# One layer of a hybrid decoder trunk: the eight turns of the last residual block ahead of their reading, sums of quarters moved in six blocks, a read of the residual asked for one group later

## The chip, the cores and the metric

The kernel runs on one core of one Trainium2 chip. A core has five engines with queues of their own: TensorE (PE; PEld is its weight load), VectorE (DVE), ScalarE (ACT), GpSimd (POOL) and SyncE (SP), which here issues most DMAs. The metric is the device time of the core in microseconds, the median of several runs.

## The reference, cut to what matters

One layer with 256 positions and 2048 channels, all in float32. The change lies at the end of the first half (output projection and residual) and in the second half (the gated MLP):

```python
def rmsnorm(x, w):
    xf = x.astype(jnp.float32)
    y = xf * lax.rsqrt(jnp.mean(xf * xf, axis=-1, keepdims=True) + EPS)
    return (y * w.astype(jnp.float32)).astype(x.dtype)
...
        mixed = jax.nn.sigmoid(g_a) * y_a + jax.nn.sigmoid(g_b) * y_b
        x = x + jnp.einsum('bsd,de->bse', mixed, w_out[l])

        h = rmsnorm(x, norm_ffn_w[l])
        gate, up = jnp.split(jnp.einsum('bsd,df->bsf', h, w_up[l]), 2, axis=-1)
        gate = causal_dwconv(gate, conv_ffn_w[l]) + conv_ffn_b[l]
        x = x + jnp.einsum('bsf,fd->bsd', jax.nn.gelu(gate, approximate=False) * up, w_down[l])
    return rmsnorm(x, norm_final_w)
```

`w_up` is 2048 x 11264 (5632 columns of gate, 5632 of up), `w_down` 5632 x 2048.

## The kernel before

**Slabs and products.** All weights stream once from memory in slabs of 256 rows by 512 columns (tile 128x2x512, 512 KB). A slab is split for TensorE: ScalarE casts it to a high half (`whi`, L285), VectorE subtracts that from the slab and keeps the rest as low half (`wlo`, L293). A product of a slab is then three kinds of matmuls into a PSUM bank: high weights by high and by low features, then low weights by high features. `weights()` hands out the next slab and first has two more slabs split (`AHEAD = 2`). There are three buffers each of `whi` and `wlo` and four of the raw slab, so a cast waits until the product three slabs back has left its buffer, and a load until the slab four loads back has been split.

**The order.** The list `srcs` fixes the order of slabs for the whole kernel. In the up projection TensorE's order is the one written (`manual_schedule`); ScalarE, VectorE, GpSimd and SyncE are put in order by a scheduler, with hints that one instruction is to come after another (`issue_after`). Each engine then executes its queue in that order. The framework keeps track of dependences by tile: a write into one half of a tile waits for earlier reads of the other half.

**The last residual block.** For each of four column groups `c` the output projection is added to the residual (L1233), and `turned_rows` turns the result: eight 128x128 transposes on TensorE against the identity (L1249), read from PSUM by ScalarE (L1254, high half of the features `fhl`) and VectorE (L1255, low half). For `c == 3` this is done inside the up projection, behind its second product, with one PSUM tile `shared` for all eight turns; there it turns four blocks, reads them in two pairs, turns the other four, reads them. The features so made (k 12 to 15, one tile) are read first by the product of the seventh slab, the fifth product after the turns.

**Blocks of the up projection.** There are eleven column groups `c`, 512 columns of gate and 512 of up. In the groups of `TWO` (1 to 7 and 9) two 1024-row chunks of the gate weights, `ch` 1 and then 0, are multiplied as two by two quarters in seven products instead of eight. The four quarters are loaded into buffers of their own (`quad_load`, L219): b11, b12, b21, b22. Sums of them are made in place by VectorE (L226): T1 = b12 - b11 into b12, T2 = b22 - T1 into b12, T3 = T2 - b11 into b11, T4 = b21 - T2 into b12. The products of a block are called by their operand and their chunk, so 21(0) is the quarter b21 of chunk 0. Around the end of one group they stand in this order, with plain products of the group before between the first ones: T1(1), 11(1), T1(0), 11(0), T2(1), T2(0), 21(1), 21(0), the eight turns of the gate (L1429), T3(1), T3(0), 22(1), 22(0), the eight turns of up, T4(1), T4(0). Two additions by VectorE bring partial results from one PSUM bank into another: L1389 (before 22 begins) and L1403 (before T4 begins). L1324 is the convolution of the gate, ScalarE's L1420 copies finished columns out of PSUM.

**When a sum is made.** `sums_behind` says behind which slab's split a sum is asked for. In the groups of `TWO`, T1(0) and T2(1) are asked for behind 11(1) and the slab after it, T2(0) behind T1(0)'s next slab, T3(1) behind the split of T2(1), T3(0) and T4(1) behind that of T2(0), T4(0) behind that of 21(1). The buffers of chunk 0 are the same four in every block, so the next block's four loads wait for this block's last reader of each.

**The down projection.** It runs in two halves of the output columns; `SEVEN = (8, 9, 10)` names three row groups that are done with seven products. The residual is read back from memory for each half (L1548): for the second half into a tile `xtl` that takes the buffer `ups`, asked for on GpSimd's queue when group 9 of that half begins.

Of the kernel before, what the change touches and what calls it, by code (L numbers as in the profile page):

```python
# [35 lines left out]
def kernel(  # L36
# [59 lines left out]
    TWO = (1, 2, 3, 4, 5, 6, 7, 9)  # L96
# [37 lines left out]
    for n, src in enumerate(srcs):  # L134
        if isinstance(src, tuple):
            what, ch = src[2:]
            if src[1] not in TWO:
                behind = {"T1": [(n, "T2", 0)], "T2": [(n, "T3", 0), (n, "T4", 0)]}.get(what, [])
            else:
                behind = {("11", 1): [(n, "T1", 0), (n + 1, "T2", 1)], ("T1", 0): [(n + 1, "T2", 0)],  # L140
                          ("T2", 1): [(n, "T3", 1), (n + 1, "T4", 1)],
                          ("T2", 0): [(n, "T3", 0), (n + 1, "T4", 0)]}.get((what, ch), [])
            for at_, sum_, of in behind:
                sums_behind.setdefault(at_, []).append((src[1], sum_, of))
# [166 lines left out]
    def pm():  # L311
        return psm.tile([P, 2, 512], F32, tag="m", name=nm("psm"))
# [914 lines left out]
    for c in range(4):  # L1227
        if c < 2:
            ps = gemm_a(at(mhi), at(mlo), KD, range(6, 8), early[c])
        else:  # L1230
            ps = gemm_a(at(mhi), at(mlo), KD)
        xs = xts[c]
        nc.vector.tensor_tensor(xs, xs, ps, op=ALU.add)  # L1233
        written = nc.gpsimd.dma_start(xt_d[:, :, c * 512 : (c + 1) * 512], xs).ins
        if c < 2:
            with tc.issue_after(written):
                residual(c + 2)
        for t in range(2):
            jk = cpool.tile([P, 512], F32, tag="sqj", name=nm("sqj"))
            nc.scalar.activation(jk, xs[:, t, :], AF.Square, accum_out=ssq4[:, t, c : c + 1])  # L1240

        def turned_rows(c=c, xs=xs):
            shared = pm() if c == 3 else None
            for k2 in range(2):
                pt = pg([P, 2, S]) if shared is None else shared[:, k2].rearrange("p (k s) -> p k s", k=2)
                for kk in range(2):
                    ks = slice((2 * k2 + kk) * P, (2 * k2 + kk + 1) * P)
                    for t in range(2):
                        nc.tensor.transpose(pt[:, kk, t * P : (t + 1) * P], xs[:, t, ks], ident)  # L1249
                for kk in range(2):  # L1250
                    k = 4 * c + 2 * k2 + kk
                    nw = vec[:, V_FFN + k : V_FFN + k + 1]
                    high, low = (both(fhl, k)[:, n, :] for n in range(2))
                    nc.scalar.activation(high, pt[:, kk, :], AF.Copy, scale=nw)  # L1254
                    nc.vector.scalar_tensor_tensor(low, pt[:, kk, :], nw, high.bitcast(F32),  # L1255
                                                   op0=ALU.mult, op1=ALU.subtract)

        if c < 3:
            turned_rows()
# [252 lines left out]
    for hf in range(2):  # L1512
# [11 lines left out]
        for n, step in enumerate(steps[hf]):  # L1524
# [16 lines left out]
            chunk, what = step[1:]  # L1541
            if what not in bank_of:
                bank_of[what] = pg()
            if what == "11" and chunk == SEVEN[1]:
                late_ = fp.tile([P, 2, 2, 512], F32, tag="ups", name="xtl") if hf else None
                for c in range(2):
                    xts[2 * hf + c] = late_[:, c] if hf else fp.tile([P, 2, 512], F32, tag=f"xt{c}", name=f"xt{c}")
                    nc.gpsimd.dma_start(xts[2 * hf + c], xt_d[:, :, (2 * hf + c) * 512 : (2 * hf + c + 1) * 512])  # L1548
# [122 lines left out]
```

## Time and profile before

| what | value |
|---|---|
| median of 3 runs | 1545.0 us (1544.96 to 1546.24) |
| the profiled execution, its own time | 1548.43 us |
| its span, first to last instruction | 1546.7 us |
| TensorE, share of the span | 99% |
| VectorE, ScalarE, GpSimd | 81%, 55%, 5% |
| mean granted TensorE clock | 0.998 |
| HBM, mean over the span | 200 GB/s |

The profile is one execution. A row of the timeline merges equal instructions that follow each other without a pause; its brackets tell how long the engine had been idle and which instruction's end let it go on. A matmul of 512 columns is shown with 0.39 us, but they are pipelined and start every 0.227 us, so lost time on TensorE is read from start to start. The granted clock is 1.00 nearly everywhere.

### The profile page before, as it was taken

What the parts mean: (1) busy time and instruction counts of PE and PEld (TensorE: products, weight loads), DVE (VectorE), ACT (ScalarE), POOL (GpSimd) and SP (SyncE); (2) the same over time, 40 slices, a digit from 0 to 9 for tenths busy, and PEclk for the clock granted to TensorE, in tenths of its full rate; (3) what the DMA queues carried; (4) which work ended last, traced back from release to release, by engine and by line L of the source; (5) the groups of instructions that cost most, each with busy time, mean ns of one, the idle gap of its engine ahead of it and who ended that gap; (6) DMA issues with size and microseconds to landing.
All of it is one profiled execution on the core that took longest, in us unless ns stands there. A gap on an engine that the chain in (4) does not pass through costs nothing.

```text
span 1546.7 us, 20222 instructions
## 1 busy us (share of the span) xinstructions
PE 1529.4 (99%) x7302; PEld 1258.7 (81%) x7302; DVE 1254.7 (81%) x1776; ACT 850.5 (55%) x1063; POOL 70.8 (5%) x90
## 2 busy tenths in 40 slices
PE   9999999999999999999999999999999999999998
PEld 8887888788888888888887888888888888888786
DVE  6789859896689868887656899999998886878785
ACT  6445446454555445454454676666666665555552
POOL 1010002000100000000100000000000000000100
PEclk9999999999999999999999999999999999999999
DMA  8776757676577756776578655666457468556652
GB/s 275 207 228 205 201 156 219 211 216 178 168 239 210 200 166 200 213 216 185 182 244 281 193 190 191 216 204 206 150 161 232 126 212 272 183 187 204 225 188 91
DMA packets 166675, 310.47 MB, mean 201 GB/s; under 512 B 19458, under 2 KB 23330, under 8 KB 166446
## 3 DMA queue, kind: packets, MB, share of 16 engines
q1 hardware_dynamic: 159456, 287.37, 60.1%
q0 software_dynamic: 5184, 18.88, 3.8%
q10 hardware_dynamic: 1934, 2.93, 0.6%
q8 instruction: 57, 0.93, 0.2%
q14 instruction: 44, 0.36, 0.1%
HBM read 301.75 MB, written 7.38 MB: 200 GB/s over the span
## 4 chain that ended last, share of the span: by engine, by line
PE 94%; DVE 2%; DMA 2%; issue 1%; ACT 1%; POOLq 0%; POOL 0%; SPq 0%; DVEq 0%; ACTq 0%
PE psg L1367 27%; PE psm L330 15%; PE psm L328 15%; PE psm L329 15%; PE psm L1352 7%; PE psg L1352 6%; PE psm L1367 2%; PE psm L474 1%; DVE wlo L293 1%; PE psm L1429 1%; PE psg L373 1%; DMA raw<-in_w_down_dram 1%; PE psg L864 1%; PE psg L866 0%; DMA vrow<-ev 0%
## 5 line engine op out<-in xcount | busy, mean ns | idle before, releaser
L285 ACT CAST whi<-raw 128x1024 fp32r<-128x1024 f32 x428 | 450.0, 1052 | 426.8 <-PE psm L329 285.2
L293 DVE TENSOR_TENSOR wlo<-raw,whi 128x1024 fp32r<-128x1024 f32 x426 | 518.2, 1221 | 150.8 <-ACT whi L285 142.9
L285 ACT CAST whi<-quad 128x1024 fp32r<-128x1024 f32 x168 | 177.1, 1054 | 139.0 <-PE psg L1367 61.5
L293 DVE TENSOR_TENSOR wlo<-quad,whi 128x1024 fp32r<-128x1024 f32 x168 | 202.6, 1222 | 36.3 <-ACT whi L285 35.4
L330 PE MATMUL psm<-wlo,xhl 128*128 128x512 f32 x432 | 169.6, 393 | 0.9 <-DVE wlo L293 0.9
L328 PE MATMUL psm<-whi,xhl 128*128 128x512 f32 x432 | 169.1, 392 | 0.0
L329 PE MATMUL psm<-whi,xhl 128*128 128x512 f32 x432 | 168.7, 391 | 0.0
L1367 PE MATMUL psg<-whi,fhl 128*128 128x512 f32 x504 | 127.4, 390 | 0.0
L1367 PEld LDWEIGHTS psg<-whi,fhl 128*128 128x128 f32 x504 | 94.5, 188 | 19.8
L330 PEld LDWEIGHTS psm<-wlo,xhl 128*128 128x128 f32 x432 | 81.1, 188 | 18.3 <-DVE wlo L293 1.7
L329 PEld LDWEIGHTS psm<-whi,xhl 128*128 128x128 f32 x432 | 81.1, 188 | 16.8
L328 PEld LDWEIGHTS psm<-whi,xhl 128*128 128x128 f32 x432 | 81.2, 188 | 16.6
L226 DVE TENSOR_TENSOR quad<-quad,quad 128x1024 f32<-128x1024 f32 x72 | 87.3, 1219 | 0.0
L1367 PE MATMUL psg<-wlo,fhl 128*128 128x512 f32 x252 | 70.6, 392 | 3.6 <-DVE wlo L293 3.6
L1367 PEld LDWEIGHTS psg<-wlo,fhl 128*128 128x128 f32 x252 | 46.8, 188 | 15.6 <-DVE wlo L293 6.2
L1367 PE MATMUL psg<-whi,ups 128*128 128x512 f32 x216 | 58.9, 395 | 0.0
L1352 PE MATMUL psm<-whi,hhi 128*128 128x512 f32 (+1 forms) x150 | 58.2, 388 | 0.0
L1352 PE MATMUL psm<-whi,hlo 128*128 128x512 f32 (+1 forms) x150 | 58.0, 386 | 0.0
L1352 PE MATMUL psm<-wlo,hhi 128*128 128x512 f32 (+1 forms) x150 | 57.5, 388 | 0.1
L1352 PE MATMUL psg<-whi,hhi 128*128 128x512 f32 (+1 forms) x130 | 50.4, 388 | 0.9 <-ACT whi L285 0.9
L328 PE MATMUL psm<-whi,mhi 128*128 128x512 f32 x128 | 50.9, 398 | 0.0
L1352 PE MATMUL psg<-whi,hlo 128*128 128x512 f32 (+1 forms) x130 | 50.0, 386 | 0.0
(432 smaller groups left out, 2932.1 us busy)
## 6 DMA issues: line engine op xcount, KB each, us to landing
raw<-in_w_in_dram SPq DMA_DIRECT2D x224, 512.0 KB, 4.2
raw<-in_w_up_dram SPq DMA_DIRECT2D x104, 512.0 KB, 4.7
quad<-in_w_up_dram SPq DMA_DIRECT2D x72, 512.0 KB, 4.5
raw<-in_w_down_dram SPq DMA_DIRECT2D x64, 512.0 KB, 4.9
raw<-in_w_out_dram SPq DMA_DIRECT2D x32, 512.0 KB, 3.8
quad<-in_w_down_dram POOLq DMA_DIRECT2D x24, 512.0 KB, 5.2
mv<-vrow SPq DMA_DIRECT2D x12, 512.0 KB, 4.8
taps<-in_conv_qkv_w_dram SPq DMA_DIRECT2D x16, 256.0 KB, 6.9
```

Of the source, the lines that this page charges most:

```text
L226: nc.vector.tensor_tensor(out_, plus_, minus_, op=ALU.subtract)
L285: nc.scalar.copy(hi, raw)
L293: last_split[0] = nc.vector.tensor_tensor(lo, raw, hi.bitcast(F32), op=ALU.subtract).ins
L328: mm(ps[:, t, :], lh(k, t), hi[:, kk, :], start=(k == 0), stop=False)
L329: mm(ps[:, t, :], ll(k, t), hi[:, kk, :], start=False, stop=False)
L330: mm(ps[:, t, :], lh(k, t), lo[:, kk, :], start=False, stop=(k == nk - 1))
L373: nc.tensor.transpose(pt[:, ff, t * P : (t + 1) * P], src[:, t, f * P : (f + 1) * P], ident)
L474: mm(ps_k0[:, t, :], part(k, t), w[:, kk, :], start=(k == 0 and w is hi and part is xh), stop=(k == KD - 1 and w is lo))
L864: mm(pg0, kq[:, h, 0, 0:P], kq[:, h, :, :], start=True, stop=True)
L1352: mm(ps[:, cs], lhs(kk), part_[:, kk, cs], start=(first and kk == 0 and n == 0), stop=(last and kk == 1 and n == 2), skip_group_check=shared)
L1367: mm(ps, lhs(kk), w[n][:, kk], start=(first and n == 0 and kk == 0 and lhs is high), stop=False, skip_group_check=True)
L1429: nc.tensor.transpose(out_[f // 2][:, f % 2, t * P : (t + 1) * P], e[:, t, f * P : (f + 1) * P], ident)
```

## The change

Three edits. In `turned_rows` all eight turns are written first and the four pairs of reads after them. In `sums_behind` the groups whose predecessor is also in `TWO` (2 to 7) get a table of their own, in which T3(1) is asked for behind the split of T2(0), T3(0) behind that of 21(0), T4(1) behind that of T3(0) and T4(0) behind that of 22(1). And the second half's read of the residual is asked for when group 10 begins, not group 9.

```diff
             if src[1] not in TWO:
                 behind = {"T1": [(n, "T2", 0)], "T2": [(n, "T3", 0), (n, "T4", 0)]}.get(what, [])
+            elif src[1] - 1 in TWO:
+                behind = {("11", 1): [(n, "T1", 0), (n + 1, "T2", 1)], ("T1", 0): [(n + 1, "T2", 0)],
+                          ("T2", 0): [(n, "T3", 1)], ("21", 0): [(n, "T3", 0)],
+                          ("T3", 0): [(n, "T4", 1)], ("22", 1): [(n, "T4", 0)]}.get((what, ch), [])
             else:
                 behind = {("11", 1): [(n, "T1", 0), (n + 1, "T2", 1)], ("T1", 0): [(n + 1, "T2", 0)],
                           ("T2", 1): [(n, "T3", 1), (n + 1, "T4", 1)],
...
             shared = pm() if c == 3 else None
+            pts = []
             for k2 in range(2):
                 pt = pg([P, 2, S]) if shared is None else shared[:, k2].rearrange("p (k s) -> p k s", k=2)
+                pts.append(pt)
                 for kk in range(2):
                     ks = slice((2 * k2 + kk) * P, (2 * k2 + kk + 1) * P)
                     for t in range(2):
                         nc.tensor.transpose(pt[:, kk, t * P : (t + 1) * P], xs[:, t, ks], ident)
+            for k2, pt in enumerate(pts):
                 for kk in range(2):
                     k = 4 * c + 2 * k2 + kk
...
-            if what == "11" and chunk == SEVEN[1]:
+            if what == "11" and chunk == SEVEN[1 + hf]:
                 late_ = fp.tile([P, 2, 2, 512], F32, tag="ups", name="xtl") if hf else None
```

The number of instructions stays the same on every engine. Lines behind the first edit have numbers 4 higher in the changed kernel, those behind the second 7 higher (L293 is L297, L1249 is L1255, L1367 is L1374).

TensorE at the turns of the last residual block, before; a row shows what an instruction writes and reads, and in brackets the engines whose semaphores it waits for (`psm_7281` is the shared tile, `xt_6774` the residual):

```order
L1249 MATMUL psm_7281<-ident,xt_6774 128x128 [waits DVE_49]
L1249 MATMUL psm_7281<-ident,xt_6774 128x128 x3
L1249 MATMUL psm_7281<-ident,xt_6774 128x128 [waits DVE_49]
L1249 MATMUL psm_7281<-ident,xt_6774 128x128 x3
L1367 MATMUL psg_7236<-whi_7239,fhl1a 128x512 [waits Activation_49]
```

And after:

```order
L1255 MATMUL psm_7281<-ident,xt_6774 128x128 [waits DVE_49]
L1255 MATMUL psm_7281<-ident,xt_6774 128x128 x7
L1374 MATMUL psg_7236<-whi_7239,fhl1a 128x512 [waits Activation_49]
L1374 MATMUL psg_7236<-whi_7239,fhl1a 128x512
L1374 MATMUL psg_7235<-whi_7239,fhl1a 128x512 x2
```

The order of matmuls is the same; the wait for VectorE in front of the fifth turn is gone.

ScalarE at the same place, before (L285 are casts of slabs, L1254 the four reads of the turned blocks, L1278 a cast of sums of features):

```order
L285 CAST whi_7300<-raw_7298 128x1024
L1254 ACTIVATE fhl_6779<-psm_7281,vec 128x256 x4
L285 CAST whi_7318<-raw_7316 128x1024
L285 CAST whi_7351<-raw_7349 128x1024
L285 CAST whi_7371<-raw_7369 128x1024
L1278 CAST ups<-sums_7338 128x1024
```

And after:

```order
L289 CAST whi_7300<-raw_7298 128x1024
L1261 ACTIVATE fhl_6779<-psm_7281,vec 128x256 x2
L289 CAST whi_7318<-raw_7316 128x1024
L1261 ACTIVATE fhl_6779<-psm_7281,vec 128x256
L289 CAST whi_7351<-raw_7349 128x1024
L1261 ACTIVATE fhl_6779<-psm_7281,vec 128x256
L289 CAST whi_7371<-raw_7369 128x1024
L289 CAST whi_7403<-raw_7401 128x1024
```

The third and fourth read now stand behind one and two casts more.

VectorE in the block at the end of group 2, which makes the products of group 3, behind the split of T2(1), before. Rows with `wlo` are splits, here of T2(0), 21(1), 21(0), T3(1), T3(0), 22(1), 22(0); rows L226 are the sums T3(1), T3(0), T4(1), T4(0):

```order
L226 TENSOR_TENSOR quad_8064<-quad_8052,quad_8064 128x1024
L293 TENSOR_TENSOR wlo_8343<-quad_8123,whi_8341 128x1024
L226 TENSOR_TENSOR quad_8125<-quad_8123,quad_8125 128x1024
L226 TENSOR_TENSOR quad_8052<-quad_8090,quad_8052 128x1024
L293 TENSOR_TENSOR wlo_8364<-quad_8090,whi_8362 128x1024
L226 TENSOR_TENSOR quad_8123<-quad_8166,quad_8123 128x1024
L293 TENSOR_TENSOR wlo_8375<-quad_8166,whi_8373 128x1024
L1389 TENSOR_TENSOR psg_8387<-psg_8290,own_8326 128x512
L293 TENSOR_TENSOR wlo_8385<-quad_8064,whi_8383 128x1024
L293 TENSOR_TENSOR wlo_8397<-quad_8125,whi_8395 128x1024
L293 TENSOR_TENSOR wlo_8418<-quad_8078,whi_8416 128x1024
L293 TENSOR_TENSOR wlo_8430<-quad_8139,whi_8428 128x1024
```

And after:

```order
L297 TENSOR_TENSOR wlo_8342<-quad_8123,whi_8340 128x1024
L230 TENSOR_TENSOR quad_8064<-quad_8051,quad_8064 128x1024
L297 TENSOR_TENSOR wlo_8362<-quad_8090,whi_8360 128x1024
L297 TENSOR_TENSOR wlo_8372<-quad_8166,whi_8370 128x1024
L230 TENSOR_TENSOR quad_8125<-quad_8123,quad_8125 128x1024
L1396 TENSOR_TENSOR psg_8385<-psg_8290,own_8326 128x512
L297 TENSOR_TENSOR wlo_8383<-quad_8064,whi_8381 128x1024
L297 TENSOR_TENSOR wlo_8395<-quad_8125,whi_8393 128x1024
L230 TENSOR_TENSOR quad_8051<-quad_8090,quad_8051 128x1024
L297 TENSOR_TENSOR wlo_8417<-quad_8078,whi_8415 128x1024
L230 TENSOR_TENSOR quad_8123<-quad_8166,quad_8123 128x1024
L297 TENSOR_TENSOR wlo_8430<-quad_8139,whi_8428 128x1024
```

The same twelve operations, with the sums spread among the splits. In both kernels L1403 (L1410 after), L1324 (L1331) and the split of T4(1) follow.

## The prediction

> **What bounds the kernel now.** I read the page first, for the share of each engine and the chain that ended last.
>
> ```profile
> span 1546.7 us, 20222 instructions
> ...
> PE 1529.4 (99%) x7302; PEld 1258.7 (81%) x7302; DVE 1254.7 (81%) x1776; ACT 850.5 (55%) x1063; POOL 70.8 (5%) x90
> ...
> PE 94%; DVE 2%; DMA 2%; issue 1%; ACT 1%; POOLq 0%; POOL 0%; SPq 0%; DVEq 0%; ACTq 0%
> ```
>
> TensorE (PE) is busy for 99% of the span and is 94% of the chain. The change removes no matmul, so all it can win is time in which PE stands still or runs slowly. The view of waits, for PE alone, lists that time: who waited for whom, then us in total, times, longest.
>
> ```profile
> PE psg L1367 <- DVE wlo L293: 3.6, 6, 0.6
> PE psm L1249 <- DVE fhl L1255: 2.5, 1, 2.5
> ...
> PE psg L1352 <- ACT whi L285: 1.1, 3, 0.6
> ```
>
> The first row is six waits in the up projection, one in each of six blocks; the second is one wait at the last residual block; the third belongs to the down projection. The three edits touch these three rows, and together the rows are 7.2 us, 0.5% of the span. I then read the timeline at each place.
>
> **Edit 1, the eight turns.** Timeline rows give start, duration, engine, line, names, and in brackets the engine's idle time and what ended it.
>
> ```profile
> 823.90 0.60 PE L1249 MATMUL psm<-ident,xt 128*128 128x128 f32 x4
> ...
> 824.27 1.23 DVE L293 TENSOR_TENSOR wlo<-raw,whi 128x1024 fp32r<-128x1024 f32 x1 [0.61 <-ACT whi L285]
> 824.54 0.47 ACT L1254 ACTIVATE fhl<-psm,vec 128x256 fp32r<-128x256 f32 x1 [0.30 <-PE psm L1249]
> ...
> 826.43 0.48 DVE L1255 SCALAR_TENSOR_TENSOR fhl<-psm,vec,fhl 128x256 fp32r<-128x256 f32 x1 [0.54 <-ACT fhl L1254]
> 826.97 0.66 PE L1249 MATMUL psm<-ident,xt 128*128 128x128 f32 x4 [2.47 <-DVE fhl L1255]
> ...
> 827.38 3.48 PE L1367 MATMUL psg<-whi,fhl1a 128*128 128x512 f32 x8
> ...
> 830.66 1.31 PE L1367 MATMUL psg<-wlo,fhl1a 128*128 128x512 f32 x4
> ...
> 831.81 2.01 PE L1367 MATMUL psg<-whi,fhl1b 128*128 128x512 f32 x8
> ```
>
> Four turns run, ScalarE and VectorE read them in two pairs, and only then do the other four turns run. Four turns take 0.41 to 0.44 us from start to start (826.97 to 827.38), so the first four were over at 824.34 and PE stood still for 2.63 us until 826.97. In the new order nothing stands between the fourth and the fifth turn; the semaphore wait there is gone. So 2.63 us go.
>
> Behind the stall a second loss follows. Eight matmuls and four more should take 12 x 0.227 us = 2.72 us; from 827.38 to 831.81 they took 4.43, 1.71 too many. The windows say why (length, busy time of the five engines, granted clock, DMA share, GB/s):
>
> ```profile
> 823.90:827.00 3.10, 0.63 (x6) 0.39 (x4) 2.10 (x3) 1.28 (x3) 0.56 (x1) 1.00 1.04 392
> 827.00:830.70 3.70, 3.70 (x13) 3.02 (x14) 0.97 (x2) 0.95 (x2) 0.00 (x0) 0.60 1.05 384
> 830.70:832.00 1.30, 1.30 (x6) 1.07 (x5) 0.00 (x0) 1.05 (x1) 0.00 (x0) 0.84 1.05 389
> ```
>
> The granted clock was halved for 0.40 x 2 x 3.70 + 0.16 x 2 x 1.30 = 3.4 us right behind the stall, which costs half of that, 1.7 us. The six waits of 0.6 us are followed by no such drop (the window of one of them, quoted under edit 2, has 1.00). So without the stall the 1.7 us should go too, in an execution that had them. [...]
>
> Can PE go on at once? The VectorE row at 824.27 is the split of the third slab ahead, so the next three products had their operands when the stall began; they last until 824.8 + 3 x 2.72 = 832.9. The casts of the fourth and fifth slab waited for PE to free a buffer, not for data:
>
> ```profile
> 830.90 1.05 ACT L285 CAST whi<-raw 128x1024 fp32r<-128x1024 f32 x1 [1.73 <-PE psg L1367]
> ...
> 833.89 1.06 ACT L285 CAST whi<-raw 128x1024 fp32r<-128x1024 f32 x1 [1.95 <-PE psg L1367]
> ```
>
> In the new order the fourth's can start when the first product's high matmuls end, 824.8 + 1.8 = 826.6. The four reads now lie between casts on ScalarE, and the product that needs them is the fifth after the turns, at 824.8 + 4 x 2.72 = 835.7. The last read stands behind the fifth slab's cast, which PE frees 2.72 later, at 829.3; with 1.05 for the cast, 0.47 for the read, and on VectorE one split (1.23) and 0.48 for its own read, it is done at about 833. It is hidden by 2.7 us. Bounds for edit 1: 0 if a new wait takes the whole stall, 4.3 if stall and gate both go.
>
> **Edit 2, the sums of quarters.** Six blocks stall alike; here is the block at 955, PE first, then VectorE and ScalarE.
>
> ```profile
> 960.41 1.07 PE L1367 MATMUL psg<-whi,ups 128*128 128x512 f32 x4
> ...
> 961.77 1.07 PE L1367 MATMUL psg<-whi,fhl1b 128*128 128x512 f32 x4
> 962.76 0.73 PE L1367 MATMUL psg<-wlo,fhl1b 128*128 128x512 f32 x2
> ...
> 965.03 0.73 PE L1367 MATMUL psg<-wlo,fhl 128*128 128x512 f32 x2 [0.62 <-DVE wlo L293]
> ...
> 971.48 0.62 PE L1367 MATMUL psg<-wlo,ups 128*128 128x512 f32 x2
> ...
> 972.74 1.17 PE L1367 MATMUL psg<-whi,fhl1b 128*128 128x512 f32 x4
> ```
>
> ```profile
> 955.80 1.23 DVE L293 TENSOR_TENSOR wlo<-quad,whi 128x1024 fp32r<-128x1024 f32 x1 [0.23 <-ACT whi L285]
> 956.95 1.22 DVE L226 TENSOR_TENSOR quad<-quad,quad 128x1024 f32<-128x1024 f32 x1
> ...
> 959.22 2.35 DVE L226 TENSOR_TENSOR quad<-quad,quad 128x1024 f32<-128x1024 f32 x2
> ...
> 963.75 1.22 DVE L293 TENSOR_TENSOR wlo<-quad,whi 128x1024 fp32r<-128x1024 f32 x1
> 964.89 0.70 DVE L1389 TENSOR_TENSOR psg<-psg,own 128x512 f32<-128x512 f32 x1
> 965.49 4.62 DVE L293 TENSOR_TENSOR wlo<-quad,whi 128x1024 fp32r<-128x1024 f32 x4
> 970.03 0.70 DVE L1403 TENSOR_TENSOR psg<-psg,own 128x512 f32<-128x512 f32 x1
> 970.63 0.48 DVE L1324 SCALAR_TENSOR_TENSOR y<-psm,cfw,y 128x255 f32<-128x255 f32 x1
> ```
>
> ```profile
> 956.15 1.05 ACT L285 CAST whi<-quad 128x1024 fp32r<-128x1024 f32 x1
> ...
> 960.25 1.06 ACT L285 CAST whi<-quad 128x1024 fp32r<-128x1024 f32 x1
> ```
>
> ```profile
> 958.00:974.00 16.00, 15.38 (x76) 12.34 (x75) 16.00 (x18) 10.96 (x13) 0.00 (x0) 1.00 0.38 113
> ```
>
> VectorE works 16.00 of 16.00 us: here it is the bound, and PE loses because four sums stand ahead of splits that PE needs sooner. A product of a quarter is six matmuls, 1.36 us (960.41 to 961.77): 0.91 for the four high ones, 0.45 for the two low ones. Eight turns take 0.8 (971.48 to 972.74, less 0.45), with 0.1 lost at their edge. Without stalls: two products from 961.77 end at 964.49, the turns of the gate at 965.4, three products at 969.5, and the low matmuls of 22(0) start at 970.4. They start at 971.48, so a block loses 1.1 us.
>
> Now the new order, row by row. Consecutive full-size VectorE operations start 1.135 us apart (956.95 and 959.22 are two steps), L1389 takes 0.60. The split of T2(0) must wait for its cast (956.15 + 1.05), so it starts at 957.24 instead of 956.95: 0.3 idle. Sum T3(1) at 958.38, split 21(1) at 959.51. Split 21(0) wants to start at 960.65 but its cast ends at 961.31 (960.25 + 1.06; ScalarE copies other results before it and waits for PE): 0.7 idle. Then sum T3(0) 962.49, L1389 963.62, splits T3(1) 964.22 and T3(0) 965.36, sum T4(1) 966.49, split 22(1) 967.63, sum T4(0) 968.76, split 22(0) 969.90 to 971.12. The two old stalls vanish (the splits of 21 end at 960.7 and 962.6, needed at 962.7 and 964.0). Splits T3(1), T3(0) and 22(1) end at 965.4, 966.6 and 968.9, needed at 966.3, 967.7 and 969.0 to 969.1. But 22(0) is needed at 970.4 and ends at 971.12: a new wait of 0.7 to 0.8. PE goes on at 971.17 instead of 971.48, 0.31 earlier. The reason is plain: a full engine that now idles 1.0 us reaches the end of the same twelve operations 1.0 later. Behind it stand L1403 (0.6), L1324 (0.4) and the split of T4(1), which ends at 973.2; PE needs it at 971.17 + 1.25 + 1.0 = 973.4, just covered. Six blocks: 6 x 0.31 = 1.9 us. Bounds: 6 x 1.1 = 6.6 if all is hidden; a loss of 2 if T4's thin cover fails by 0.6 us in each block.
>
> **Edit 3, the late read of the second half.** The program order on GpSimd's queue is the same before and after: these reads stand between the same two quarter loads, and wait for the same product.
>
> ```profile
> 1444.74 1.44 POOL L1548 DMA_DIRECT2D xtl<-xtd  x2 [6.67 <-PE psm L1352]
> ```
>
> No row moves on any other engine there either. I count 0; the 1.1 us of L1352 stay.
>
> **The sum.** Against the profiled execution: 1546.7 - 2.6 - 1.7 - 1.9 = 1540.5 us of span. That execution took 1548.43 us, 3.4 over the median of the timed runs, 1545.0. Whether those paid the gate can't be seen, so I count half of it: 1545.0 - 2.6 - 1.9 - 0.85 = 1539.6 us.
>
> **Rivals.** *The VectorE stall only moves* and edit 2 wins nothing, since T3(1), 22(1) and T4 are covered by 0.1 to 0.9 us: 1540.7 with the gate counted, 1542.4 without. *VectorE catches up entirely*, because ScalarE's casts come earlier than I put them: 6.6 instead of 1.9, 1534.9. Against it: both casts that make it idle wait for PE. *A new wait at the residual block*: the fifth slab lands late, as the stall no longer gives the DMA time (its share is 1.04 to 1.05 there). The last read then comes late with its cast; from a landing after 832 on PE waits again, up to all of 2.6 + 0.85: 1545.0 - 1.9 = 1543.1. Against it: the cast at 833.89 waited for PE, with its data there for up to 2 us.
>
> *Slower*: SyncE's queue is in order. In a block's end stand four quarter loads for the next block, then four plain slabs.
>
> ```profile
> 965.00 8.77 SPq L219 DMA_DIRECT2D quad<-in_w_up_dram  x4
> 974.93 5.38 SPq L205 DMA_DIRECT2D raw<-in_w_up_dram  x4
> ```
>
> The first of the four waited for split 21(0) (964.97); its buffer is now read by sum T4(0) last, which I put at 970.0. Four loads bunch behind it, and the slabs behind them. At the 384 to 392 GB/s above a load of 0.52 MB takes 1.35 us, so four are through by 975.4, and the slabs' own condition decides, the split of the first slab in use, 1.0 late like all of VectorE here. The first of these slabs is cast at 980.36 and read by PE at 986.46:
>
> ```profile
> 980.36 1.05 ACT L285 CAST whi<-raw 128x1024 fp32r<-128x1024 f32 x1 [1.25 <-PE psg L1367]
> ```
>
> ```profile
> 986.46 1.98 PE L1367 MATMUL psg<-whi,fhl2a 128*128 128x512 f32 x8
> ```
>
> The cast waited for PE, not for the load, and ends 5 us ahead of its use, so the queue decides only from about 5 us of delay on. (In block 8 two quarter loads also change places in this queue; I count 0 for it.) If it did decide, each further us costs six: 1.25 a block gives 1545.0 - 2.6 - 0.85 + 7.5 = 1549.0.
>
> **Chances.** Forecast 0.50 (1538.8 to 1540.5, with the gate in all of the timed runs or in none); stall only moves 0.22; catches up 0.10; new residual wait 0.10; slower 0.08. 0.2% is 3.1 us, about what a measurement tells from no change: faster means below 1541.9. Faster: 0.475 + 0.125 + 0.10 = 0.70; same 0.22; slower 0.08. The range leaves out the slower rival and the far end of catching up: 1536.0 to 1544.0; the forecast's own is 1538.0 to 1541.0.
>
> **What would show it.** In the new profile: eight turns in one row of about 0.9 us, no wait on L1255's successor, granted clock 1.00 from 823 to 836. In each of the six blocks the waits of 21(1) and 21(0) gone and one wait of 0.6 to 0.7 before the low matmuls of 22(0), VectorE idle by about 0.3 and 0.7 before the splits of T2(0) and 21(0). POOL's rows and L1352's 1.1 us as before. Wrong: a wait at L1374 within 12 us behind the turns, or six waits of 1 us and more.

## The result and the profile after

The changed kernel takes 1542.1 us (median of 12 runs, 1539.8 to 1543.0), the kernel before 1545.4 beside it (12 runs, 1544.1 to 1546.2): a ratio of 0.9977, 95% interval 0.9968 to 0.9986, so 3.3 us less, with 2.2 to 4.9 in the interval. The forecast was 1539.6 us: the result lies in the range of 1536.0 to 1544.0, but above the forecast's own 1538.0 to 1541.0. By the number alone it could as well be the rival in which the second edit wins nothing (1542.4 without the half clock behind the stall, which the sum of the forecast calls the gate); the profiles below have to tell the two apart. In the profiled executions the span went from 1546.7 to 1540.8 us; the forecast for that pair was 1540.5.

The head of the page of the changed kernel, then its waits of TensorE (engine, tile, line, what ended the wait: us in total, times, longest):

```profile
span 1540.8 us, 20209 instructions
...
PE 1526.0 (99%) x7302; PEld 1257.4 (82%) x7302; DVE 1253.4 (81%) x1776; ACT 849.8 (55%) x1063; POOL 70.8 (5%) x90
```

```profile
PE psg L1374 <- DVE wlo L297: 4.0, 7, 0.6
PE psm L334 <- DVE wlo L297: 1.9, 3, 1.2
...
PE psg L1359 <- ACT whi L289: 0.4, 1, 0.4
```

The 13 instructions fewer than before are semaphore instructions of the sequencers of VectorE (12) and ScalarE (1); the working ones are as many as before. The wait of 2.5 us at the turns is gone. The six waits of the up projection are still there, and a seventh beside them: 4.0 us against 3.6. The wait at L1359 (L1352 before) fell from 1.1 to 0.4, and at L334, in the first half of the program where nothing was changed, it is 1.9 where it was 1.2.

Since both kernels run the same matmuls in the same order, I laid the two traces side by side, matmul by matmul, and took the time from the start of one to the start of the next in each. That gives where the 5.9 us of the two profiles went (a table worked out from the traces, not a view of the profile; negative is faster):

| stretch (us of the kernel before) | before | after | difference |
|---|---|---|---|
| 1 to 815, nothing changed | 814.0 | 814.9 | +0.9 |
| 815 to 840, the turns | 25.17 | 20.85 | -4.32 |
| 910 to 1173, the six blocks | 262.49 | 261.69 | -0.80 |
| 1440 to 1480, down projection | 39.89 | 38.55 | -1.34 |
| the rest | 397.45 | 397.17 | -0.28 |

So the forecast for the span came out nearly right by luck, since errors cancel: the blocks gave 0.8 instead of 1.9, the down projection, for which I had counted 0, gave 1.3, and the first part, where nothing was changed, took 0.9 more.

**The turns** in the timeline of the changed kernel, and windows over it (length, busy time of the five engines, granted clock, DMA share, GB/s):

```profile
823.89 1.08 PE L1374 MATMUL psg<-wlo,fhl 128*128 128x512 f32 x4
...
824.81 1.04 PE L1255 MATMUL psm<-ident,xt 128*128 128x128 f32 x8
...
825.60 2.07 PE L1374 MATMUL psg<-whi,fhl1a 128*128 128x512 f32 x8
...
833.57 0.47 DVE L1262 SCALAR_TENSOR_TENSOR fhl<-psm,vec,fhl 128x256 fp32r<-128x256 f32 x1
...
836.58 1.75 PE L1374 MATMUL psg<-whi,fhl 128*128 128x512 f32 x7
```

```profile
824.80:828.40 3.60, 3.60 (x21) 3.13 (x20) 2.18 (x3) 1.98 (x4) 0.28 (x1) 1.00 1.05 397
828.40:832.00 3.60, 3.60 (x17) 2.99 (x16) 2.97 (x5) 1.90 (x4) 0.00 (x0) 1.00 1.04 383
```

Eight turns in one row take 0.79 us from start to start, TensorE is busy all of the time behind them, and the clock is 1.00. The fourth read ends at 834.04 and its product starts at 836.58, 2.5 us later.

**A block.** TensorE first (the low matmuls of 21(0), then the last two products of quarters before the turns, 22(1) and 22(0)), then VectorE from the split of T2(1) on:

```profile
960.30 0.62 PE L1374 MATMUL psg<-wlo,fhl 128*128 128x512 f32 x2
...
965.27 0.62 PE L1374 MATMUL psg<-wlo,ups 128*128 128x512 f32 x2
965.74 1.08 PE L1374 MATMUL psg<-whi,ups 128*128 128x512 f32 x4
967.43 0.73 PE L1374 MATMUL psg<-wlo,ups 128*128 128x512 f32 x2 [0.61 <-DVE wlo L297]
968.00 1.03 PE L1436 MATMUL psm<-ident,e 128*128 128x128 f32 x8
```

```profile
953.05 2.35 DVE L297 TENSOR_TENSOR wlo<-quad,whi 128x1024 fp32r<-128x1024 f32 x2
955.32 1.22 DVE L230 TENSOR_TENSOR quad<-quad,quad 128x1024 f32<-128x1024 f32 x1
956.46 2.37 DVE L297 TENSOR_TENSOR wlo<-quad,whi 128x1024 fp32r<-128x1024 f32 x2
...
966.16 1.22 DVE L297 TENSOR_TENSOR wlo<-quad,whi 128x1024 fp32r<-128x1024 f32 x1
```

The waits at the products of 21 are gone, and the one forecast wait stands before the low matmuls of 22(0): 0.61 by the row, 0.78 from start to start (965.74 + 0.91 = 966.65 without it). Two low matmuls behind a wait take 0.57 (967.43 to 968.00), two that waited for nothing 0.47 (965.27 to 965.74), so the wait costs 0.88 in all.

**What is new: late slabs.** Two casts of slabs on ScalarE in the changed kernel, at the same place of two neighbouring blocks, then VectorE's split behind each:

```profile
1020.51 1.05 ACT L289 CAST whi<-raw 128x1024 fp32r<-128x1024 f32 x1 [1.18 <-DMA raw<-in_w_up_dram]
...
1065.43 1.05 ACT L289 CAST whi<-raw 128x1024 fp32r<-128x1024 f32 x1 [2.58 <-DMA raw<-in_w_up_dram]
```

```profile
1021.59 1.22 DVE L297 TENSOR_TENSOR wlo<-raw,whi 128x1024 fp32r<-128x1024 f32 x1 [0.82 <-ACT whi L289]
...
1066.51 1.23 DVE L297 TENSOR_TENSOR wlo<-raw,whi 128x1024 fp32r<-128x1024 f32 x1 [2.22 <-ACT whi L289]
```

In each of the six blocks ScalarE now waits 1.2 to 2.6 us for a slab; in the kernel before these casts waited for TensorE, and none waited 0.7 or more for a slab. The blocks are 43.5 us apart, and the split at 1066.51 comes 44.92 after its fellow. The block behind it took 44.17 us, 0.66 more than the others: its 22(1) waited too, the seventh wait.

```profile
1096.37 0.73 PE L1374 MATMUL psg<-wlo,ups 128*128 128x512 f32 x2 [0.34 <-DVE wlo L297]
```

The slab itself was not what TensorE waited for: its cast ended at 1066.48, and its product began at 1069.53 without a wait. As I read it, VectorE, with next to no free time in these blocks, carried the delay on to the splits of the quarters.

### The profile page after: what moved, and what is told of

Its sections match the earlier page's. It is cut to its first block, busy times and chain, and to the rows that moved or that the text cites. A ratio compares the mean times of both kernels' runs of the same rounds, so it can differ in the third digit from the quotient of the medians.

```text
span 1540.8 us, 20209 instructions
## 1 busy us (share of the span) xinstructions
PE 1526.0 (99%) x7302; PEld 1257.4 (82%) x7302; DVE 1253.4 (81%) x1776; ACT 849.8 (55%) x1063; POOL 70.8 (5%) x90
## 4 chain that ended last, share of the span: by engine, by line
PE 92%; DVE 4%; issue 2%; DMA 1%; ACT 0%; POOL 0%; POOLq 0%; DVEq 0%; ACTq 0%
PE psg L1374 25%; PE psm L334 15%; PE psm L332 14%; PE psm L333 14%; PE psm L1359 7%; PE psg L1359 7%; DVE wlo L297 3%; PE psm L1374 2%; PE psm L478 1%; PE psg L377 1%; DVE quad L230 1%; PE psm L1436 1%; DMA vrow<-ev 1%; PE psg L868 1%; DMA mv<-vrow 1%
## 5 line engine op out<-in xcount | busy, mean ns | idle before, releaser
L297 DVE TENSOR_TENSOR wlo<-raw,whi 128x1024 fp32r<-128x1024 f32 x426 | 517.3, 1220 | 151.2 <-ACT whi L289 146.2
L297 DVE TENSOR_TENSOR wlo<-quad,whi 128x1024 fp32r<-128x1024 f32 x168 | 202.6, 1219 | 36.2 <-ACT whi L289 35.3
L334 PE MATMUL psm<-wlo,xhl 128*128 128x512 f32 x432 | 169.5, 393 | 1.6 <-DVE wlo L297 1.6
L1374 PE MATMUL psg<-whi,fhl 128*128 128x512 f32 x504 | 127.1, 389 | 0.0
L1374 PEld LDWEIGHTS psg<-whi,fhl 128*128 128x128 f32 x504 | 94.4, 188 | 19.5
L334 PEld LDWEIGHTS psm<-wlo,xhl 128*128 128x128 f32 x432 | 81.1, 188 | 19.0 <-DVE wlo L297 2.4
L1374 PE MATMUL psg<-wlo,fhl 128*128 128x512 f32 x252 | 69.9, 389 | 0.0
L1374 PE MATMUL psg<-whi,ups 128*128 128x512 f32 x216 | 58.9, 394 | 0.0
L1359 PE MATMUL psm<-whi,hhi 128*128 128x512 f32 (+1 forms) x150 | 58.1, 387 | 0.0
L1359 PE MATMUL psm<-whi,hlo 128*128 128x512 f32 (+1 forms) x150 | 57.9, 386 | 0.0
L1359 PE MATMUL psm<-wlo,hhi 128*128 128x512 f32 (+1 forms) x150 | 57.4, 387 | 0.1
L1374 PEld LDWEIGHTS psg<-wlo,fhl 128*128 128x128 f32 x252 | 47.3, 188 | 9.8
L1359 PE MATMUL psg<-whi,hhi 128*128 128x512 f32 (+1 forms) x130 | 50.3, 387 | 0.4 <-ACT whi L289 0.4
L1359 PE MATMUL psg<-whi,hlo 128*128 128x512 f32 (+1 forms) x130 | 50.0, 386 | 0.0
```

The lines of the kernel that those rows point to most:

```text
L297: last_split[0] = nc.vector.tensor_tensor(lo, raw, hi.bitcast(F32), op=ALU.subtract).ins
L334: mm(ps[:, t, :], lh(k, t), lo[:, kk, :], start=False, stop=(k == nk - 1))
L1359: mm(ps[:, cs], lhs(kk), part_[:, kk, cs], start=(first and kk == 0 and n == 0), stop=(last and kk == 1 and n == 2), skip_group_check=shared)
L1374: mm(ps, lhs(kk), w[n][:, kk], start=(first and n == 0 and kk == 0 and lhs is high), stop=False, skip_group_check=True)
```

## The experiments

Each is compared with the kernel before, run beside it: 1545.05 us for the first four (22 runs), 1545.7 for the next four (16), 1546.1 for the last four (14). The three sets ran on three chips, so runs of different sets are compared by what they gain over the kernel before.

### One edit at a time

The first edit alone:

```diff
+            pts = []
...
+                pts.append(pt)
...
+            for k2, pt in enumerate(pts):
                 for kk in range(2):
                     k = 4 * c + 2 * k2 + kk
```

> Only the first edit: the eight turns of the last residual block in a row; sums and residual read as before. The prediction's reasons: the wait of 2.63 us at the turns goes and nothing takes its place within 12 us behind them, so the time is 2.6 us below before (in rounds 1542.3 to 1543.1 where before has 1545.4). If the timed executions of before also pay the half-clock stretch of 1.7 us that its profiled one shows, 4.3 below instead (about 1541.1). Rival, the stall only moves: within 0.5 of before, with a wait of 2 us or more at L1374 behind the turns. In the profile no half-clock row between 815 and 840. The six blocks keep their 1.07 us of waits each.

1540.8 us, ratio 0.9968 (0.9956 to 0.9980). TensorE's waits:

```profile
PE psg L1370 <- DVE wlo L293: 3.7, 6, 0.6
PE psm L330 <- DVE wlo L293: 1.4, 1, 1.4
...
PE psg L1355 <- ACT whi L285: 0.2, 1, 0.2
```

No wait at the turns, none behind them; the stretch from 815 to 840 takes 20.85 us to the hundredth as in the changed kernel. The gain of 4.2 by the medians is near the value with the gate, and the interval (3.1 to 6.8 us) lies above 2.6, though not by much. The wait at L1355 is small here as well, and the second edit, alone, tells the rest:

```diff
+            elif src[1] - 1 in TWO:
+                behind = {("11", 1): [(n, "T1", 0), (n + 1, "T2", 1)], ("T1", 0): [(n + 1, "T2", 0)],
+                          ("T2", 0): [(n, "T3", 1)], ("21", 0): [(n, "T3", 0)],
+                          ("T3", 0): [(n, "T4", 1)], ("22", 1): [(n, "T4", 0)]}.get((what, ch), [])
```

> Only the second edit: the table of the six blocks; turns and residual read as before. From the profile of the changed kernel: a block's two waits (1.07 us with their edges) become one of 0.88, and a block is 0.2 to 0.25 us shorter, so 1.2 to 1.5 us below before over six blocks. Rival, late slabs take it back (the changed kernel lost 0.5 in its sixth block behind a slab that came 1.4 us late): 0.5 or less below before. If the two edits add up, this and the first alone make the 3.3 us that both together gave. The wait of 2.5 us at the turns stays.

1545.4 us, ratio 0.9996 (0.9987 to 1.0005): no gain that can be told. Its six blocks take 261.18 us where the old table takes 262.2 to 262.5, and the stall with the half clock (0.50 from 828.37 to 831.78) is in its profile. ScalarE's waits for slabs, 1.1 to 2.1 us in each block, are in it too, where the first edit alone had one in six blocks, so they belong to the second.

The third alone:

```diff
-            if what == "11" and chunk == SEVEN[1]:
+            if what == "11" and chunk == SEVEN[1 + hf]:
```

> Only the third edit: the residual's second half is asked for one group later. Reasons of the prediction: the order of no engine but SyncE's names changes, so the same time as before within 0.5 us, and the waits of 1.1 us at L1352 stay as they are in before. Rival: the 0.7 us that the changed kernel waits less at that line in the down projection comes from this edit; then this run is 0.7 below before and its waits there are 0.4. It is also a second look at the turns with the stall in place: if a stall always costs the half-clock stretch, the profile shows one of about 3.4 us again; if it hangs on phase, it may be missing.

1545.1 us, ratio 0.9996 (0.9988 to 1.0005). The wait in the down projection is 0.2 here, but so it is in the first edit's run, and in that of the second there is none; a later profile of the kernel before had none either. The 1.1 us was that one execution's and no edit's. The other half of the question gave more: here the stall stood and the half-clock stretch did not. Pieces of 3.413 us, which is how long the half clock lasted in the profile of the kernel before, laid from the first granted full clock on, in that profile and then in this one:

```profile
824.28:827.70 3.42, 0.95 (x9) 0.69 (x7) 2.09 (x3) 0.98 (x3) 0.18 (x1) 1.00 1.05 392
827.70:831.11 3.41, 3.41 (x10) 2.67 (x9) 0.97 (x2) 1.12 (x3) 0.00 (x0) 0.50 1.05 385
831.11:834.52 3.41, 3.41 (x16) 2.81 (x15) 2.46 (x4) 1.46 (x2) 0.00 (x0) 1.00 0.69 242
```

```profile
822.57:825.99 3.42, 2.05 (x12) 1.49 (x10) 2.46 (x5) 1.53 (x2) 0.72 (x1) 1.00 1.05 404
825.99:829.40 3.41, 2.31 (x12) 2.01 (x13) 1.07 (x4) 1.42 (x3) 0.00 (x0) 1.00 1.04 374
829.40:832.81 3.41, 3.41 (x16) 2.82 (x16) 2.49 (x4) 1.46 (x2) 0.00 (x0) 1.00 1.05 389
```

Before, the whole wait lay in one piece (busy 0.95 of 3.42), and the next piece ran at 0.50. Here it was cut in two (2.05 and 2.31 busy), and the clock stayed at 1.00.

### VectorE's idle time filled

The changed kernel with another table: T3's sums where they were before, T4's late.

```diff
-                          ("T2", 0): [(n, "T3", 1)], ("21", 0): [(n, "T3", 0)],
+                          ("T2", 1): [(n, "T3", 1)], ("T2", 0): [(n, "T3", 0)],
                           ("T3", 0): [(n, "T4", 1)], ("22", 1): [(n, "T4", 0)]}.get((what, ch), [])
```

> The changed kernel with another table for the six blocks: the sums of T3 stand directly behind the splits of T2(1) and T2(0), as in before, so that VectorE has work while it would idle 0.6 us ahead of the split of 21(0); the sums of T4 stay late (behind T3(0) and 22(1)). By the rows of the changed kernel (block at 1036) the splits of 21(1) and 21(0) end at 1045.2 and 1046.3 and are needed at 1046.0 and 1047.3; the split of 22(0) ends at 1053.7 instead of 1054.4 and is needed at 1053.7. If VectorE's idle 0.6 to 0.7 is what the new wait is made of, 0.7 to 0.9 us go in each of the six blocks: 4 to 5 us below the changed kernel, about 1537.5, and the waits before the low matmuls of 22(0) are under 0.15. Rival: the block is held by something else behind the sums (the casts or the loads of quarters); then it stays within 1 us of the changed kernel, 1541 to 1543.

1537.9 us, ratio 0.9944 (0.9932 to 0.9957), by the medians 7.2 below before and 2.8 to 3.8 more than the changed kernel's gain in its two sets; the 4 to 5 expected were a little too much. TensorE's row for L1374, three waits in place of seven:

```profile
PE psg L1374 <- DVE wlo L297: 1.4, 3, 0.5
```

They are not all under 0.15 as expected. The six blocks take 258.9 us against 261.7, with one block of 44.17 behind a slab 2.6 us late among them; the first, with no wait at all, takes 42.64. So the new wait of the changed kernel was made by its order of sums, and most of it goes with another.

### The table taken out, two other orders, and the changed kernel again

The changed kernel without the second edit (the first and third alone):

> The changed kernel without its second edit (turns in a row and the residual's second half, old table of sums). Theory, the table gains 0.2 us in each of six blocks and nothing else: this run is 1.2 us above the changed kernel run beside it. Rival, the table gives back what it gains by late slabs: within 0.5 of it. The first edit alone had 1540.8 where the changed kernel had 1542.1 on another day; if that holds, this run is 1 us below, and the table costs more than it gains.

1542.5 us, ratio 0.9978 (0.9969 to 0.9986); the changed kernel beside it, below, 1541.4. That is 1.1 more, as the theory had it, though the difference is within what two such medians scatter; the rival from the first sets (1 us the other way) is not borne out.

A third table:

```diff
-                          ("T2", 0): [(n, "T3", 1)], ("21", 0): [(n, "T3", 0)],
-                          ("T3", 0): [(n, "T4", 1)], ("22", 1): [(n, "T4", 0)]}.get((what, ch), [])
+                          ("T2", 1): [(n, "T3", 1)], ("T2", 0): [(n, "T3", 0)],
+                          ("21", 0): [(n, "T4", 0)], ("22", 1): [(n, "T4", 1)]}.get((what, ch), [])
```

> The changed kernel with a third table: T3 sums behind the splits of T2(1) and T2(0) as in the table that fills VectorE's idle time, sum T4(0) directly behind the split of 21(0), sum T4(1) behind that of 22(1). It is sum T4(0) that lets the first of the next four quarter loads start (in the changed kernel the load starts at 1053.34, the sum ends at 1053.28), and SyncE's queue has the slabs behind them. By the changed kernel's rows the sum ends 5.9 us earlier than there (1047.4 in place of 1053.3). Theory: no wait of PE over 0.2 in the six blocks, ScalarE waits less than 0.7 us for slabs in them (1.2 to 2.6 in the changed kernel), blocks of 42.5 us: 1 to 2 us below the table that only fills the idle time (1537.9), so 1536 to 1537. Rival: the splits of T3 come late, since two sums stand ahead of them; then a wait of 0.3 or more before the low matmuls of T3(1), and no gain over 1537.9.

1537.1 us, ratio 0.9941 (0.9928 to 0.9955), 8.6 below before. TensorE's waits in the blocks are down to 0.5 us in three, but the blocks take 42.6 to 43.4 us, 257.8 in all, and ScalarE still waits 1.0 to 1.8 us for slabs in five of them: that part of the expectation failed. Two blocks take 42.6 us, four 0.3 to 0.8 more. From start to start these four lose 0.3 to 0.4 us each at the low matmuls of 22(0), where the rows show waits of 0.17 or none, so the wait of the changed kernel has become shorter there but is not gone. The longest block (43.44) stands behind the latest slab (1.82), and one of the two shortest (42.61) behind the least late one (0.97); but one of the four (43.11) has no such slab ahead of it by the rows, so that late slabs make the rest of the wait is likely, not shown. Nor can it be told whether this table is better than the one before it: they gain 7.0 to 11.1 us and 6.6 to 10.5 by their intervals.

The changed kernel with two loads of quarters swapped:

```diff
-        ch, i = n // 4, (1, 0, 3, 2)[n % 4]
+        ch, i = n // 4, (0, 1, 3, 2)[n % 4]
```

> The changed kernel with the first two quarter loads of each four in the other order, so that the load whose buffer is freed by the split of T3(0) (about 1049.9 in the block at 1036) goes first, and the one that waits for sum T4(0) second. Theory, the late slabs come from that queue: the four loads start 3 us earlier, ScalarE's waits for slabs in the six blocks fall from 1.2 to 2.6 us to under 1, and no block is lengthened by a late slab (the changed kernel lost 0.65 in its block at 1085): 0.5 to 1 us below the changed kernel run beside it. Rival, the slabs are held by the transfers themselves or by their own buffers: the waits stay as they are, and so does the time.

1540.7 us, ratio 0.9968 (0.9956 to 0.9981), 0.7 below the changed kernel beside it, which the scatter does not tell from nothing. Its waits for slabs are 0.8 to 2.4 us, so the reason was wrong. SyncE's queue in the block at 1036 shows why: four quarter loads, then four slabs, in the run without the table, in the changed kernel, and in this one:

```profile
1047.38 8.77 SPq L219 DMA_DIRECT2D quad<-in_w_up_dram  x4
1057.30 5.34 SPq L205 DMA_DIRECT2D raw<-in_w_up_dram  x4
```

```profile
1053.34 4.73 SPq L223 DMA_DIRECT2D quad<-in_w_up_dram  x4
1059.22 4.55 SPq L209 DMA_DIRECT2D raw<-in_w_up_dram  x4
```

```profile
1048.47 8.17 SPq L223 DMA_DIRECT2D quad<-in_w_up_dram  x4
1057.80 4.55 SPq L209 DMA_DIRECT2D raw<-in_w_up_dram  x4
```

The swap let the first load go 4.9 us earlier, but the fourth goes at 1056.64 (1048.47 + 8.17) against 1058.07, and these 1.4 us are what this whole execution was ahead there. The fourth waits for the split of T4(0):

```profile
1053.89 2.35 DVE L297 TENSOR_TENSOR wlo<-quad,whi 128x1024 fp32r<-128x1024 f32 x2
```

```profile
1055.32 2.35 DVE L297 TENSOR_TENSOR wlo<-quad,whi 128x1024 fp32r<-128x1024 f32 x2
```

These end at 1056.24 here and 1057.67 in the changed kernel, 0.4 before the fourth load in both. So it is the end of VectorE's chain that holds the queue, not sum T4(0).

The changed kernel itself:

> The changed kernel itself, beside the other three on the same chip: 1542.1 within 0.7. Its profile shows a second time whether the slab of the block at 1085 comes late (44.17 us for that block, 43.5 for the others) or whether the late one falls elsewhere, and whether the two waits before 815 us (282 and 460, 1.9 us in all) are the same.

1541.4 us, ratio 0.9972 (0.9960 to 0.9983). The block at 1085 takes 43.52 us here, and no other is longer than 43.53. ScalarE's wait is put down to a slab's load in three of the six blocks (1.3 to 2.2 us) and to TensorE in the other three (1.5 each). So a slab so late that TensorE pays came in one of two profiles. The waits at L334 before 815 are 1.4 us in two, not 1.9 in three.

### The stall lengthened, and two more profiles of the kernel before

```diff
-                    nc.vector.scalar_tensor_tensor(low, pt[:, kk, :], nw, high.bitcast(F32),
-                                                   op0=ALU.mult, op1=ALU.subtract)
+                    for _ in range(3 if c == 3 and k2 == 0 else 1):
+                        nc.vector.scalar_tensor_tensor(low, pt[:, kk, :], nw, high.bitcast(F32),
+                                                       op0=ALU.mult, op1=ALU.subtract)
```

> The kernel before with VectorE's two reads of the first four turns each done three times, so that the wait of PE at the turns is about 1.9 us longer (four more of 0.48 us): 4.5 in place of 2.63. Theory: the wait lies wholly on the path, so 1.9 us more; and the half-clock stretch hangs on how much of the wait falls into one piece of a fixed grid of 3.413 us (tripped with 2.64 us inside one piece in two profiles, not tripped with 1.53 and 1.11 in two pieces). A wait of 4.5 us puts at least 2.25 into one piece, so it should trip nearly always: 2.0 to 2.7 us above the kernel before, and the profile has half-clock behind the turns; stretch 815 to 840 of about 27 us, against 25.2 and 23.6. Rival: part of the wait is hidden elsewhere; then less than 1.5 us are added.

1549.1 us, ratio 1.0022 (1.0012 to 1.0031), 3.0 above before by the medians. The wait is 4.6 us (4.72 from start to start), the stretch 28.15 us. Pieces laid in the same way:

```profile
823.16:826.57 3.41, 0.35 (x4) 0.11 (x1) 2.68 (x5) 1.03 (x3) 0.00 (x0) 1.00 1.04 395
826.57:829.98 3.41, 1.92 (x7) 1.73 (x8) 1.62 (x4) 0.47 (x1) 0.00 (x0) 0.50 1.05 387
829.98:833.40 3.42, 3.42 (x10) 2.65 (x9) 0.70 (x2) 1.25 (x2) 0.00 (x0) 0.50 0.71 252
833.40:836.81 3.41, 3.41 (x17) 2.78 (x16) 2.78 (x5) 1.21 (x2) 0.00 (x0) 1.00 0.16 23
```

Two pieces at 0.50 instead of one, which I had not foreseen: 5.34 us of half clock behind the wait cost 2.67. With the wait, 4.72 + 2.67 = 7.39 over the stretch without a stall, and 28.15 - 20.85 = 7.30 was measured.

> The kernel before itself, one look. By the fixed grid: if the wait at the turns (2.64 us) lies whole in one piece of the grid of 3.413 us that starts with the first granted full clock, the half-clock stretch is there and the stretch 815 to 840 takes 25.2 us; if it is cut so that no piece holds more than 1.6, the stretch takes 23.6. The rest of the program within 1 us of the other profiles up to 815 (713.0 to 714.9).

> As the look before it: 25.2 us for the stretch 815 to 840 with the wait whole in one piece of the grid, 23.6 with the wait cut. Between these, the first look at a cut of about 2 us in one piece would show where the line lies.

The first took 1548.3 us with a stretch of 25.09, the second 1542.7 with 23.55. Pieces of the first, then of the second:

```profile
824.35:827.76 3.41, 1.07 (x7) 0.69 (x5) 2.02 (x3) 1.76 (x3) 0.52 (x1) 1.00 1.04 402
827.76:831.17 3.41, 3.27 (x10) 2.79 (x11) 1.05 (x3) 0.95 (x2) 0.00 (x0) 0.50 1.05 381
```

```profile
820.47:823.88 3.41, 2.20 (x12) 1.63 (x10) 2.30 (x5) 1.53 (x2) 0.72 (x1) 1.00 1.05 398
823.88:827.30 3.42, 2.16 (x12) 1.87 (x13) 1.15 (x3) 1.39 (x3) 0.00 (x0) 1.00 1.04 377
```

Both fell as expected: with 1.07 us of busy time in the piece of the wait the next ran at 0.50, with 2.20 and 2.16 in two pieces the clock stayed at 1.00. A cut near 2 us did not come up, so these two do not show where a line lies.

Nor is the rest of one program one time: these two executions of the same kernel are 5.6 us apart, 1.5 of it at the turns and 2.8 before 815, where fourteen profiles range from 812.2 to 814.9 us (the 713.0 to 714.9 above should have read 813.0 to 814.9).

Last, the third table and the swapped loads together:

> The table with sum T4(0) behind the split of 21(0), with the first two quarter loads of each four in the other order as well. From the other two runs: the order of the loads moved the first load 5 us but not the last, which waits for the split of T4(0), so the slabs start where they did. Theory: no more than 0.5 us from 1537.1 either way. Rival: earlier quarter loads make room in the transfers and blocks go from 42.4 to 43.4 us down to 42.4 each: 1.5 us below, 1535.6.

1537.6 us, ratio 0.9947 (0.9933 to 0.9960). The six blocks take 258.0 us, as with the table alone: nothing won, as the theory had it.

## Why the prediction was right and where it was not

**The stall at the turns: right, in mechanism and size.** Forecast 2.63 us. In the two profiles whose stall paid no half clock the stretch takes 23.55 and 23.56 us, in all with the turns in a row 20.85: 2.7 us. None of the rivals at this place came: no wait follows, the fourth read had 2.5 us to spare where I had put 2.7.

**The gate: right, and now shown.** I took half of 1.7 us without knowing how many of the timed runs paid it, and no run shows these 0.85 us as such. What the profiles show is this: the stretch with half clock takes 25.1 to 25.2 us, so it costs 1.5 to 1.6, and it fell in three of the five profiles that have the stall of 2.6 us: 1.0 on average by that count, against 0.85. The timed runs of the experiments carry a mean granted clock of three digits: of 52 runs of the kernel before, 20 have 0.999 (1544.5 us on average) and 32 have 0.998 or 0.997 (1546.3 us), while the kernels with the turns in a row have 0.999 in 41 of 55 runs and never less than 0.998. So some timed runs paid and others did not; by these shares about half of them did, which is an estimate.

**The six blocks: right in mechanism, wrong in size.** This is the term that was mis-sized: 6 x 0.31 = 1.9 us forecast, while the three profiles with the table and no slab that hurt have 261.06 to 261.18 us, those with the old table 262.3 on average: 1.2 us, 0.2 a block. The step that failed is the price of the new wait. I took 0.7 to 0.8 for it, from start to start, and set it against 1.1 for the two old ones, which held the slower matmuls behind each wait: laid side by side, the old waits are 0.20 and 0.87 with these edges, 1.07. The new wait has such an edge too: 0.78 + 0.10 = 0.88 against 1.07 leaves 0.19. The wait itself came where I put it and as long as I put it. The timed runs do not show this gain by themselves (1545.4 us against 1545.05 for the second edit alone; 1.1 us between two kernels that differ by it, within their scatter), so the 1.2 us rest on the starts of matmuls in the profiles.

The idle time by which I explained it was half right. The idle 0.3 before T2(0) came in one of the six blocks, as 0.2, and that before 21(0) in three (0.57 to 0.61 us, forecast 0.7). In the others VectorE had lost the time earlier, waiting 1.5 to 2.2 us for the cast of a late slab, and entered the chain later. Either way it reached the split of 22(0) 5.4 us behind the start of the gate's turns in five blocks, and 6.1 in the one behind the latest slab. That filling the time takes most of the wait away is shown by the other two tables: 0.4 to 0.6 us a block.

**The rival I called slower was half there.** I argued that SyncE's queue decides only from 5 us of delay on, since the slab's cast ended 5 us ahead of its use. The slabs did come late, by the reason that I gave (the end of VectorE's chain comes 1.0 later). But the measure of cover was wrong. A cast that is late holds the split behind it, and behind that everything VectorE has to do; with VectorE full, 1.4 us of delay took 0.66 from TensorE, not the excess over 5. It happened in one of twelve blocks of the two profiles of the changed kernel, and in one of six with the table that fills the idle time, both times behind a slab for which ScalarE waited 2.6 us; in the changed kernel waits up to 1.9 us cost nothing. That the delay goes by way of VectorE is read from the rows; no run moves that slab alone.

**The residual's second half: right.** No gain, no loss (0.9996, 0.9988 to 1.0005). But "the 1.1 us of L1352 stay" was wrong: 0 to 0.6 us in every other run, with and without the edit. I read a scatter of one execution as a property of the kernel.

**The sum.** With the measured terms it should have been 1545.4 - 2.7 - 1.0 - 1.2 = 1540.5. The changed kernel had 1542.1 and, in the second set, 1541.4 against 1545.7. The first interval (2.2 to 4.9 us) just holds these 4.9 us, the second (2.6 to 6.2) holds them well. What remains, 1.6 us in the first set, I cannot place: a slab that hurts (0.66) would be a part, and the first 815 us, where nothing was changed, scatter by 2.8 us from profile to profile. It was not settled whether the kernel's other placement of loads makes that part slower: seven profiles with a new table have 813.9 us there on average, seven with the old one 813.5, which is within that scatter.

## What to carry to other kernels

Price a wait with its edges on both sides of the comparison; here the 0.10 us left out was a third of the gain forecast for a block. On an engine that is busy all the time, the slack of an operation is not the time until its own result is used but what the operations behind it on that engine have to spare, so a late load can be paid for at another place (here 1.4 us of delay took 0.66 from TensorE, though the slab's cast ended 3.05 us ahead of its product); and moving work later only helps if other work that is ready fills the hole, as the two other tables showed (7.2 and 8.6 us below before, where the change won 3.3 to 4.3). One profile tells one execution: a wait that is not in a second profile of the same kernel is no ground for a term of a sum.

## What the runs showed of the hardware

The granted clock behind the stall at the turns, profile by profile, in the pieces of 3.413 us above. In the first profile of the kernel before the half clock begins 822.61 us behind the first full clock, which is 241 such pieces, and lasts one; the piece ahead of it held 0.95 us of busy time on TensorE. With the second edit alone and in the first of the two later profiles of the kernel before a piece with 0.95 and one with 1.07 us were followed by one at 0.50 as well. With the third edit alone (2.05 and 2.31 us) and in the second later profile (2.20 and 2.16) the wait was cut in two, and the clock stayed at 1.00. Ahead of the half clock of the long wait stands a piece with 0.35 us; of the two at 0.50 the first held 1.92 us of busy time and the second was full, and the next had 1.00. So the same stall of 2.6 us cost 2.7 us in the two profiles in which it was cut in two and 4.2 to 4.3 in the three in which it lay in one piece, and the one of 4.7 us cost 7.3. These are six profiles of one place in one program; a rule for other stalls was not shown.
